# Strassen FFN weights: sums W11+W12 and W11+W12+W22 built by loads and accumulating transfers, W11 loaded by itself

## The chip, the cores and the metric

One core of a Trainium2 chip runs the whole program. The metric is the device time of one execution in microseconds (us), the median of the runs shown. Beside the plain runs there is one profiled execution, from which all rows come. Engines are named as in the profile: PE (TensorE, matmuls), DVE (VectorE), ACT (ScalarE), POOL (GpSimd), SP (SyncE). SP issues plain loads, POOL issues transfers that add to their destination while they write it (accumulating transfers).

## What is computed

A two-layer encoder trunk over two groups of 256 tokens with 1024 channels. Each layer is a half-step SwiGLU FFN, a mixer (gated DeltaNet and differential attention) and a second half-step FFN, so the program has four FFNs. All are in float32. The change touches the FFN alone, in its two products with the gate weights wg and the up weights wu (each 1024 x 2816):

```python
def swiglu(x, wg, wu, wd):
    return (jax.nn.silu(x @ wg) * (x @ wu)) @ wd

x = x + 0.5 * swiglu(rmsnorm(x, ffn1_norm[l]), ffn1_wg[l], ffn1_wu[l], ffn1_wd[l])
```

## The kernel before

Each float32 matmul is three matmuls of a high and a low part: high weights with high and low activations, low weights with high activations. `split` (L218) makes the two parts of a weight tile: ACT casts it to the high part `wh` (L226), DVE subtracts that from the tile for the low part `wl` (L228). The parts live in a pool `pw` of four buffer pairs.

**The FFN.** The 22 column blocks (of 128) are worked through in three groups, (0, 8), (8, 16) and (16, 22). Two blocks at a time make 256 gate and 256 up columns for 512 tokens. The first pair of an FFN uses plain products; each later pair is one call of `seven` (L393), which takes gate and up columns together as a 2 x 2 block matrix and needs seven products instead of eight, by Strassen's scheme: rows 0 to 511 of wg are W11, of wu W12; rows 512 to 1023 of wg are W21, of wu W22. There are ten calls in an FFN (three, four and three in the groups), 40 in the program. After a group comes its part of the down projection with wd (`rowproj`, L298 to L304), some 44 us for eight blocks.

**One call of `seven`** (L393 to L443). A product is 24 matmuls of 256 columns (L389 to L391). In the order of the code the products use W11 (with X11, activations), W11+W12+W22 (called t2), W11+W12, W12+W22 (t3, in the tiles P and M), W21 (in R and S), W22, and W11+W12+W22+W21 (t2 again, after W21 was added). C holds combinations of the activations, made once for each FFN by `combos` (L355 to L374): four tiles of tag u are filled by an SP load of the high parts (L361) and a POOL accumulation of the low parts (L362), then combined by DVE (L363) and split by ACT and DVE (L370, L371).

**How the weights come in before the change.** SP loads W11 into one half of a `raw` tile and W22 into the other (L399, L400), W22 once more in halves into P and M (L403), and W21 in halves into R and S (L407). POOL adds W12 to P and M (L404). W11 is split for the first product; then POOL adds W12 to it in place (L412), which therefore has to wait for that split. DVE adds W22 to the result for t2 (L414).

**What sets the order.** The program is scheduled at build time by a planner that orders every engine's instructions by their priority and by when they can run in its own model; on the chip each engine and each issuing queue then keeps that order. `high_priority(offset=AHEAD)` with AHEAD = 1500 moves loads, splits and the two sums far ahead of their place in the code. How far they really go ahead is set by buffers: two for `raw` (which the loads of wd use too), two each for the tags P, M, R and S, 14 for the tag u. Of these 14, four hold the tokens x, two a call's results hh and hl (until the down projection has read them), one a t2, and for a while four the combinations.

Of the kernel before, what the change touches and what calls it, by code (L numbers as in the profile page):

```python
# [17 lines left out]
ALU = mybir.AluOpType  # L18
# [3 lines left out]
P = 128  # L22
# [12 lines left out]
AHEAD = 1500  # L35
# [25 lines left out]
def trunk_kernel(tc, I, O, dbg=None, depth=DEPTH, stop=None):  # L61
    nc = tc.nc
    with ExitStack() as st:
# [15 lines left out]
        def nm(s):  # L79
            cnt[0] += 1  # L80
            return f"{s}{cnt[0]}"

        def u(shape=(P, 2, TOK), dt=F32):
            return pu.tile(list(shape), dt, tag="u", name=nm("u"))
# [4 lines left out]
        def tmp(shape=(P, TOK)):  # L89
            return pt.tile(list(shape), F32, tag="t", name=nm("t"))  # L90

        def dtmp(tag, shape=(P, H, P)):
            return pd.tile(list(shape), F32, tag=tag, name=nm(tag))
# [4 lines left out]
        def bank(k, shape=(P, TOK)):  # L98
            return {"f": psf, "a": psx, "d": psd}[k].tile(list(shape), F32, tag="b", name=nm("ps"))
# [7 lines left out]
        V, A, G_, T = nc.vector, nc.scalar, nc.gpsimd, nc.tensor  # L107
# [110 lines left out]
        def split(rv, dst=None, share=False, off=AHEAD):  # L218
            shp = list(rv.shape)
            if dst is None:  # L220
                hi = pw.tile(shp, F32R, tag="whi", name=nm("wh"))
                lo = pw.tile(shp, F32R, tag="wlo", name=nm("wl"))
            else:
                hi, lo = dst
            with tc.high_priority(offset=off):
                A.copy(hi, rv)  # L226
                turn[0] += 1
                (G_ if share and turn[0] % 2 else V).tensor_tensor(lo, rv, hi.bitcast(F32), op=ALU.subtract)  # L228
            return hi, lo
# [109 lines left out]
        def ffn(wg, wu, wd, xT, after, extra=None, norm=None):  # L339
# [12 lines left out]
            X11, X12 = [[t[:, k, g0] for t in xT] for k in (low, high)]  # L352
            C = {}
# [22 lines left out]
            def parts_of(pieces):  # L376
                hi = pw.tile([P, 4, 256], F32R, tag="whi", name=nm("wh"))
                lo = pw.tile([P, 4, 256], F32R, tag="wlo", name=nm("wl"))
                n = 4 // len(pieces)
                for i, r in enumerate(pieces):  # L380
                    split(r, (hi[:, n * i:n * i + n, :], lo[:, n * i:n * i + n, :]))
                return hi, lo

            def product(ps, w, act, start=True):
                (wh, wl), (ch, cl) = w, act
                for j in range(2):
                    m, o = slice(j * P, (j + 1) * P), ps[:, j, :]
                    for k in range(4):
                        T.matmul(o, wh[:, k, m], ch[:, k, :], start=start and j + k == 0, stop=False, skip_group_check=True)  # L389
                        T.matmul(o, wh[:, k, m], cl[:, k, :], start=False, stop=False, skip_group_check=True)  # L390
                        T.matmul(o, wl[:, k, m], ch[:, k, :], start=False, stop=k == 3, skip_group_check=True)  # L391

            def seven(f, hh, hl):  # L393
                c = slice(f * P, f * P + 256)
                rows = lambda w, k0, n: w[k0 * P:(k0 + n) * P, c].rearrange("(k p) n -> p k n", p=P)
                with tc.high_priority(offset=AHEAD):
                    r = pr.tile([P, 2048], F32, tag="raw", name=nm("raw")).rearrange("p (q k n) -> p q k n", q=2, k=4)
                    w11, w22 = r[:, 0], r[:, 1]
                    nc.sync.dma_start(w11, rows(wg, 0, 4))  # L399
                    nc.sync.dma_start(w22, rows(wu, 4, 4))  # L400
                    t3 = [dtmp(n, (P, 2, 256)) for n in "PM"]
                    for i, t in enumerate(t3):
                        nc.sync.dma_start(t, rows(wu, 4 + 2 * i, 2))  # L403
                        G_.dma_start(t, rows(wu, 2 * i, 2), accum_op=ALU.add)  # L404
                    w21 = [dtmp(n, (P, 2, 256)) for n in "RS"]
                    for i, t in enumerate(w21):
                        nc.sync.dma_start(t, rows(wg, 4 + 2 * i, 2))  # L407
                sq_ = (P, 2, 256)
                X, E, Z = bank("f", sq_), bank("d", sq_), bank("a", sq_)
                product(X, parts_of([w11]), X11)  # L410
                with tc.high_priority(offset=AHEAD):
                    G_.dma_start(w11, rows(wu, 0, 4), accum_op=ALU.add)  # L412
                    t2 = u((P, 4, 256))
                    V.tensor_tensor(t2, w11, w22, op=ALU.add)  # L414
                p1s, G = dtmp("C", sq_), dtmp("E", sq_)
                A.copy(p1s, X)
                product(E, parts_of([t2]), C[6])
                V.tensor_tensor(G, E, p1s, op=ALU.subtract)
                product(Z, parts_of([w11]), C[5])
                product(E, parts_of(t3), C[7], False)  # L420
                H, y22 = dtmp("B", sq_), tmp(sq_)
                V.tensor_tensor(H, E, p1s, op=ALU.subtract)
                V.tensor_tensor(y22, Z, H, op=ALU.add)
                product(X, parts_of(w21), X12, False)
                s0 = tmp(sq_)
                A.activation(s0, X, AF.Silu)
                with tc.high_priority(offset=AHEAD):
                    for i, t in enumerate(w21):
                        V.tensor_tensor(t2[:, 2 * i:2 * i + 2, :], t2[:, 2 * i:2 * i + 2, :], t, op=ALU.add)
                product(Z, parts_of([w22]), C[3], False)  # L430
                V.tensor_tensor(G, Z, G, op=ALU.add)
                V.tensor_tensor(s0, s0, G, op=ALU.mult)
                product(E, parts_of([t2]), C[4], False)
                y21 = dtmp("B", sq_)
                V.tensor_tensor(y21, p1s, E, op=ALU.subtract)
                A.activation(y21, y21, AF.Silu)
                V.tensor_tensor(y22, y21, y22, op=ALU.mult)
                for v, g in ((s0, g0), (y22, g1)):
                    hi, lo = hh[-1][:, :, g], hl[-1][:, :, g]
                    A.copy(hi, v)  # L440
                    V.tensor_tensor(lo, v, hi.bitcast(F32), op=ALU.subtract)

            for f0, f1 in ((0, 8), (8, 16), (16, 22)):  # L443
                hh, hl = [], []
                for f in range(0, f1 - f0, 2):
                    hh.append(u(dt=F32R))
                    hl.append(u(dt=F32R))
                    if f0 + f:
                        seven(f0 + f, hh, hl)
                        continue  # L450
                    bs = [bank_alt() for _ in range(4)]
                    if norm is not None:
                        ws = []
                        norm(0)
                        for i, (b, rv) in enumerate(zip(bs, raw0)):
                            hi = pw.tile([P, 8, P], F32R, tag="whi", name=nm("wh"))
                            lo = pw.tile([P, 8, P], F32R, tag="wlo", name=nm("wl"))
                            if i:
                                k = (3, 7, 7)[i - 1]
                                A.copy(hi[:, 0, :1], xT[0][:, k, :1])  # L460
                                V.tensor_copy(lo[:, 0, :1], xT[1][:, k, :1])
                            ws.append(split(rv, (hi, lo), off=0 if i else AHEAD))
                            proj(b, ws[-1], xT, 0, 256)
                        norm(1, [w[0][:, 0, :1].bitcast(F32) for w in ws])
                        for b, w in zip(bs, ws):
                            proj(b, w, xT, 256, 512)
                    else:
                        gs, us = wcols(wg, 0), wcols(wu, 0)
                        for g in range(2):
                            for b, w in zip(bs, (gs[0], us[0], gs[1], us[1])):  # L470
                                proj(b, w, xT, g * 256, g * 256 + 256)
                    combos()
                    for j in range(2):
                        gate(bs[2 * j], bs[2 * j + 1], f + j, hh, hl)
# [733 lines left out]
```

## Time and profile before

| | us |
|---|---|
| median of 3 runs | 2539.91 |
| lowest and highest run | 2536.48 and 2541.99 |
| the profiled execution | 2534.26 |
| its span, first to last instruction | 2532.1 |

| engine | busy us | share of the span |
|---|---|---|
| PE | 2357.6 | 93% |
| DVE | 1498.2 | 59% |
| ACT | 1000.4 | 40% |
| POOL | 415.7 | 16% |

The mean granted clock of TensorE is 0.96 of full speed. Transfers move 301.59 MB, 119 GB/s over the span. Matmuls are pipelined and overlap in the records (a matmul of 256 columns stands with 0.28 us while the next one starts 0.12 us later), so the busy time of PE tells little; the distance of the starts does. DMA-issuing instructions are not counted as busy time of an engine.

### The profile page before, as it was taken

Reading aid. Unit: us, or ns where it says so; the run is one execution under the profiler, and the core shown is the slowest. Engines: PE = TensorE matmul, PEld = TensorE weight load, DVE = VectorE, ACT = ScalarE, POOL = GpSimd, SP = SyncE. Lnnn points to the kernel's source line nnn. Section 1 sums busy time; section 2 is a strip of 40 time slices with the busy share of each in tenths; the row PEclk is TensorE's granted clock in tenths of the full one; section 3 lists DMA queues with packets and bytes.
Section 4 is the critical chain, followed back from the end, with each engine's and each line's share of the span. In section 5 each row is a group of like instructions: output and inputs, shape, how many; then the busy total and the mean of one; then the engine's idle time right before and its main releaser. Section 6 shows DMA issues by size and latency. Waiting matters only on the chain.

```text
span 2532.1 us, 36917 instructions
## 1 busy us (share of the span) xinstructions
PE 2357.6 (93%) x14923; PEld 2133.0 (84%) x14923; DVE 1498.2 (59%) x2304; ACT 1000.4 (40%) x1864; POOL 415.7 (16%) x371
## 2 busy tenths in 40 slices
PE   6899999999999979999978989999999999799998
PEld 5888888877799878888878888988878988788897
DVE  4646565577665456564646474655776553656555
ACT  4423344643433334342433242447344333333333
POOL 2101010023351010110011010001333401101000
PEclk8899999999999989999989999999999999899999
DMA  9446435641124375453466454357221245544542
GB/s 228 116 119 132 117 93 183 154 119 57 59 67 142 110 149 142 107 138 98 125 134 139 117 115 124 83 178 182 89 80 46 80 151 136 121 119 111 132 99 76
DMA packets 274842, 301.59 MB, mean 119 GB/s; under 512 B 20589, under 2 KB 240001, under 8 KB 274672
## 3 DMA queue, kind: packets, MB, share of 16 engines
q1 hardware_dynamic: 217888, 230.36, 29.4%
q0 software_dynamic: 56608, 68.68, 16.2%
q8 instruction: 117, 1.92, 0.3%
q14 instruction: 53, 0.43, 0.1%
q10 hardware_dynamic: 176, 0.20, 0.0%
HBM read 271.11 MB, written 11.30 MB: 112 GB/s over the span
## 4 chain that ended last, share of the span: by engine, by line
PE 75%; DVE 11%; DMA 6%; ACT 4%; issue 3%; POOL 1%; SPq 1%; POOLq 0%; DVEq 0%; ACTq 0%
PE ps L389 10%; PE ps L391 10%; PE ps L390 10%; PE ps L298 7%; PE ps L299 7%; PE ps L300 7%; PE ps L241 4%; PE ps L240 4%; PE ps L242 4%; DVE wl L228 2%; DMA u<-xth 2%; ACT wh L226 2%; PE ps L859 1%; DMA v<-gcd 1%; PE ps L956 1%
## 5 line engine op out<-in xcount | busy, mean ns | idle before, releaser
L226 ACT CAST wh<-raw 128x1024 fp32r<-128x1024 f32 x326 | 340.6, 1049 | 584.3 <-PE ps L390 213.2
L228 DVE TENSOR_TENSOR wl<-raw,wh 128x1024 fp32r<-128x1024 f32 x314 | 388.3, 1239 | 285.2 <-ACT wh L226 278.0
L389 PE MATMUL ps<-xth,wh 128*128 128x256 f32 x1280 | 373.2, 292 | 60.7 <-ACT wh L226 58.9
L391 PE MATMUL ps<-xth,wl 128*128 128x256 f32 x1280 | 366.2, 286 | 9.6 <-DVE wl L228 9.6
L390 PE MATMUL ps<-xtl,wh 128*128 128x256 f32 x1280 | 367.8, 287 | 0.0
L389 PE MATMUL ps<-v,wh 128*128 128x256 f32 x960 | 292.7, 305 | 72.5 <-ACT wh L226 70.1
L240 PE MATMUL ps<-xth,wh 128*128 128x512 f32 (+1 forms) x928 | 326.8, 361 | 6.0 <-ACT t L499 2.0
L241 PE MATMUL ps<-xtl,wh 128*128 128x512 f32 (+1 forms) x928 | 329.9, 361 | 1.0 <-DVE xtl L287 1.0
L242 PE MATMUL ps<-xth,wl 128*128 128x512 f32 (+1 forms) x928 | 327.4, 358 | 0.0
L389 PEld LDWEIGHTS ps<-xth,wh 128*128 128x128 f32 x1280 | 251.2, 196 | 68.7 <-ACT wh L226 67.2
L391 PE MATMUL ps<-v,wl 128*128 128x256 f32 x960 | 289.0, 301 | 0.0
L390 PE MATMUL ps<-v,wh 128*128 128x256 f32 x960 | 288.3, 300 | 0.0
L389 PEld LDWEIGHTS ps<-v,wh 128*128 128x128 f32 x960 | 202.1, 210 | 79.1 <-ACT wh L226 75.8
L298 PE MATMUL ps<-wh,u 128*128 128x512 f32 x672 | 261.8, 390 | 0.0
L299 PE MATMUL ps<-wl,u 128*128 128x512 f32 x672 | 261.6, 389 | 0.0
L300 PE MATMUL ps<-wh,u 128*128 128x512 f32 x672 | 259.8, 389 | 0.0
L391 PEld LDWEIGHTS ps<-xth,wl 128*128 128x128 f32 x1280 | 249.1, 195 | 11.0 <-DVE wl L228 11.0
L390 PEld LDWEIGHTS ps<-xtl,wh 128*128 128x128 f32 x1280 | 251.9, 197 | 0.0
L390 PEld LDWEIGHTS ps<-v,wh 128*128 128x128 f32 x960 | 202.2, 211 | 0.4
L391 PEld LDWEIGHTS ps<-v,wl 128*128 128x128 f32 x960 | 202.3, 211 | 0.2
L240 PEld LDWEIGHTS ps<-xth,wh 128*128 128x128 f32 x928 | 174.9, 191 | 32.3 <-ACT xth L286 2.6
L241 PEld LDWEIGHTS ps<-xtl,wh 128*128 128x128 f32 x928 | 177.2, 191 | 24.2 <-DVE xtl L287 1.4
(350 smaller groups left out, 4292.9 us busy)
## 6 DMA issues: line engine op xcount, KB each, us to landing
raw<-in_w_in_dram SPq DMA_DIRECT2D x44, 1024.0 KB, 5.3
raw<-in_ffn_wd_dram SPq DMA_DIRECT2D x40, 1024.0 KB, 6.6
raw<-in_ffn_wg_dram SPq DMA_DIRECT2D x40, 512.0 KB, 4.6
raw<-in_ffn_wu_dram SPq DMA_DIRECT2D x40, 512.0 KB, 5.5
raw<-in_ffn_wu_dram POOLq DMA_DIRECT2D x40, 512.0 KB, 6.0
M<-in_ffn_wu_dram SPq DMA_DIRECT2D x40, 256.0 KB, 2.9
P<-in_ffn_wu_dram SPq DMA_DIRECT2D x40, 256.0 KB, 2.8
M<-in_ffn_wu_dram POOLq DMA_DIRECT2D x40, 256.0 KB, 7.8
```

The source lines that it names most:

```text
L226: A.copy(hi, rv)
L228: (G_ if share and turn[0] % 2 else V).tensor_tensor(lo, rv, hi.bitcast(F32), op=ALU.subtract)
L240: T.matmul(o, wh[:, k, m], xh[:, k, c0:c1], start=k == 0, stop=False)
L241: T.matmul(o, wh[:, k, m], xl[:, k, c0:c1], start=False, stop=False)
L242: T.matmul(o, wl[:, k, m], xh[:, k, c0:c1], start=False, stop=k == n - 1)
L298: T.matmul(ps, sh[:, a], wh, start=k == 0, stop=False)
L299: T.matmul(ps, sh[:, a], wl, start=False, stop=False)
L300: T.matmul(ps, sl[:, a], wh, start=False, stop=k == nk - 1)
L389: T.matmul(o, wh[:, k, m], ch[:, k, :], start=start and j + k == 0, stop=False, skip_group_check=True)
L390: T.matmul(o, wh[:, k, m], cl[:, k, :], start=False, stop=False, skip_group_check=True)
L391: T.matmul(o, wl[:, k, m], ch[:, k, :], start=False, stop=k == 3, skip_group_check=True)
L859: T.matmul(pp[:, h, :], lhs[:, h, :], rhs[:, h, :], start=True, stop=True)
```

## The change

W11 no longer shares a buffer with W11+W12. The half of the `raw` tile where W11 stood (now `t1_`) receives a load of W11 and, as soon as that has landed, POOL's accumulation of W12. W11 by itself is loaded again, in halves, into two tiles of the tag S, and split half by half. The sum t2 is no longer made by DVE: a tile of tag u receives a load of W22 and then two accumulations by POOL, of W12 and of W11. W21 moves from the tags R and S into two tiles of the tag R. For each call this makes nine loads on SP (of 0.26 or 0.52 MB) where there were six, with 3.1 MB instead of 2.1, and five accumulations on POOL where there were three, with 2.1 MB instead of 1.05; one DVE instruction of 128 x 1024 elements (L414) goes.

```diff
                 with tc.high_priority(offset=AHEAD):
                     r = pr.tile([P, 2048], F32, tag="raw", name=nm("raw")).rearrange("p (q k n) -> p q k n", q=2, k=4)
-                    w11, w22 = r[:, 0], r[:, 1]
-                    nc.sync.dma_start(w11, rows(wg, 0, 4))
+                    w11, w22, t1_ = [dtmp("S", (P, 2, 256)) for _ in range(2)], r[:, 1], r[:, 0]
+                    nc.sync.dma_start(t1_, rows(wg, 0, 4))
                     nc.sync.dma_start(w22, rows(wu, 4, 4))
+                    G_.dma_start(t1_, rows(wu, 0, 4), accum_op=ALU.add)
+                    for i, t in enumerate(w11):
+                        nc.sync.dma_start(t, rows(wg, 2 * i, 2))
+                    t2 = u((P, 4, 256))
+                    nc.sync.dma_start(t2, rows(wu, 4, 4))
+                    G_.dma_start(t2, rows(wu, 0, 4), accum_op=ALU.add)
+                    G_.dma_start(t2, rows(wg, 0, 4), accum_op=ALU.add)
                     t3 = [dtmp(n, (P, 2, 256)) for n in "PM"]
                     for i, t in enumerate(t3):
                         nc.sync.dma_start(t, rows(wu, 4 + 2 * i, 2))
                         G_.dma_start(t, rows(wu, 2 * i, 2), accum_op=ALU.add)
-                    w21 = [dtmp(n, (P, 2, 256)) for n in "RS"]
+                    w21 = [dtmp("R", (P, 2, 256)) for _ in range(2)]
                     for i, t in enumerate(w21):
                         nc.sync.dma_start(t, rows(wg, 4 + 2 * i, 2))
                 sq_ = (P, 2, 256)
                 X, E, Z = bank("f", sq_), bank("d", sq_), bank("a", sq_)
-                product(X, parts_of([w11]), X11)
-                with tc.high_priority(offset=AHEAD):
-                    G_.dma_start(w11, rows(wu, 0, 4), accum_op=ALU.add)
-                    t2 = u((P, 4, 256))
-                    V.tensor_tensor(t2, w11, w22, op=ALU.add)
+                product(X, parts_of(w11), X11)
                 p1s, G = dtmp("C", sq_), dtmp("E", sq_)
                 A.copy(p1s, X)
                 product(E, parts_of([t2]), C[6])
                 V.tensor_tensor(G, E, p1s, op=ALU.subtract)
-                product(Z, parts_of([w11]), C[5])
+                product(Z, parts_of([t1_]), C[5])
```

## Rows read from the trace of the kernel before

**Rows 1.** The page, part 4: shares of the chain that ended last, by engine.
```profile
PE 75%; DVE 11%; DMA 6%; ACT 4%; issue 3%; POOL 1%; SPq 1%; POOLq 0%; DVEq 0%; ACTq 0%
```

**Rows 2.** Waits of PE: who waited for whom, us in total, times, longest us.
```profile
PE ps L389 <- ACT wh L226: 129.0, 55, 17.0
```

**Rows 3.** Timeline of PE at a hand-over: start us, us, instruction, count [idle before, releaser].
```profile
1060.16 0.28 PE L390 MATMUL ps<-xtl,wh 128*128 128x256 f32 x1
1060.28 0.28 PE L391 MATMUL ps<-xth,wl 128*128 128x256 f32 x1
1062.18 0.38 PE L389 MATMUL ps<-v,wh 128*128 128x256 f32 x1 [1.62 <-ACT wh L226]
...
1063.92 0.41 PE L390 MATMUL ps<-v,wh 128*128 128x256 f32 x1
1064.13 0.41 PE L391 MATMUL ps<-v,wl 128*128 128x256 f32 x1
```

**Rows 4.** Windows of sevens: bounds, us, engines' busy us, PEclk, DMA share, GB/s; three sums.
```profile
906.20:993.80 87.60, 66.78 (x506) 65.06 (x505) 58.21 (x70) 35.92 (x48) 11.64 (x10) 0.88 0.59 124
...
sum 358.60, PE 268.26 PEld 261.24 DVE 233.42 ACT 146.88 POOL 48.29; mean PE 67.06 PEld 65.31 DVE 58.36 ACT 36.72 POOL 12.07
...
sum 380.30, PE 347.91 PEld 342.51 DVE 242.70 ACT 153.53 POOL 54.29; mean PE 86.98 PEld 85.63 DVE 60.68 ACT 38.38 POOL 13.57
...
sum 279.20, PE 259.10 PEld 255.54 DVE 178.93 ACT 119.03 POOL 27.89; mean PE 64.77 PEld 63.88 DVE 44.73 ACT 29.76 POOL 6.97
```

**Rows 5.** Windows of shorter stretches, columns as in rows 4.
```profile
1030.00:1040.00 10.00, 10.00 (x56) 8.71 (x55) 8.33 (x11) 3.19 (x4) 0.00 (x0) 1.00 0.00 0
...
1062.20:1087.10 24.90, 22.21 (x168) 21.79 (x168) 17.20 (x22) 10.73 (x16) 3.69 (x3) 0.93 0.57 127
...
1070.00:1080.00 10.00, 10.00 (x85) 10.00 (x85) 4.89 (x6) 2.83 (x4) 3.43 (x3) 1.00 0.85 202
```

**Rows 6.** Timelines of DVE and POOL ahead of the same hand-over.
```profile
1050.90 1.21 DVE L228 TENSOR_TENSOR wl<-raw,wh 128x1024 fp32r<-128x1024 f32 x1
...
1059.30 1.22 DVE L414 TENSOR_TENSOR u<-raw 128x1024 f32<-128x1024 f32 x1
...
1052.41 1.30 POOL L412 DMA_DIRECT2D raw<-in_ffn_wu_dram  x1 [7.66 <-DVE wl L228]
```

**Rows 7.** DMA issues: transfer, queue, count, KB each, median us from issue to landing.
```profile
raw<-in_ffn_wg_dram SPq DMA_DIRECT2D x40, 512.0 KB, 4.6
...
raw<-in_ffn_wu_dram POOLq DMA_DIRECT2D x40, 512.0 KB, 6.0
```

**Rows 8.** Timelines of POOL and DVE ahead of a second stretch's first seven.
```profile
1023.86 1.30 POOL L412 DMA_DIRECT2D raw<-in_ffn_wu_dram  x1 [37.85 <-DVE wl L228]
...
1029.84 1.22 DVE L414 TENSOR_TENSOR u<-raw 128x1024 f32<-128x1024 f32 x1 [6.28 <-DMA raw<-in_ffn_wu_dram]
```

**Rows 9.** The page, part 3: queue of SP, queue of POOL: packets, MB, share of 16 engines.
```profile
q1 hardware_dynamic: 217888, 230.36, 29.4%
q0 software_dynamic: 56608, 68.68, 16.2%
```

**Rows 10.** Timelines of DVE (split of combinations) and PE in a first stretch.
```profile
929.67 2.35 DVE L371 TENSOR_TENSOR v<-u,v 128x1024 fp32r<-128x1024 f32 x2
...
946.86 0.28 PE L391 MATMUL ps<-xth,wl 128*128 128x256 f32 x1
```

**Rows 11.** DMA queues from 880 to 915 us, columns as in rows 9.
```profile
q0 software_dynamic: 3027, 3.00, 57.9%
q1 hardware_dynamic: 4622, 4.54, 45.3%
```

**Rows 12.** Timelines of DVE and PE at the start of that first stretch.
```profile
914.03 1.23 DVE L363 TENSOR_TENSOR u<-u,u 128x1024 f32<-128x1024 f32 x1 [12.14 <-DMA u<-xtl]
...
920.30 0.58 PE L389 MATMUL ps<-xth,wh 128*128 128x256 f32 x1 [11.05 <-ACT wh L226]
...
924.45 0.58 PE L391 MATMUL ps<-xth,wl 128*128 128x256 f32 x1 [1.58 <-DVE wl L228]
```

## The prediction

> **What bounds the kernel now.** The page first: three quarters of the chain that ended last are TensorE's own matmuls [rows 1]; a gain must come out of the rest. Next, what TensorE waits for: one entry stands far above all others, 129.0 us in 55 waits of the first matmul of a product for a high part that ScalarE makes at L226 [rows 2]. Third, where these waits lie: the windows of the twelve stretches of sevens (three in each FFN, one for each group of columns before its down projection). Full speed is a matmul every 0.12 us, as at the end of a seven [rows 3], so a seven of 168 matmuls takes 20.16 us. The first stretches of the four FFNs (three sevens each, 60.5 us at full speed) take 358.6 us instead of 241.9, 116.7 too much; the second (four sevens each) 380.3 instead of 322.6, 57.7 too much; the third (three each) 279.2 instead of 241.9, 37.3 too much [rows 4].
>
> In the second and third stretches that loss of 95.0 us lies at the 20 places where one seven hands over to the next, 4.75 us each. Fourth, the timeline at one of them. TensorE has its last matmul at 1060.28, its next at 1062.18, and then another short wait [rows 3]; after the gap matmuls start 0.21 us apart instead of 0.12 [rows 3]. The granted clock is 0.93 over a seven with such a gap and 1.00 from 1070 to 1080, where there is none [rows 5]: behind the idle time TensorE runs for a while at the lower of its two levels (1.2 instead of 2.4 GHz), and this adds about as much as the gap.
>
> The gap is the end of one chain. VectorE finishes the split of W11 at 1052.11; only then may POOL add W12 to the same buffer (issued 1052.41) [rows 6], which lands 6.0 us later at the median [rows 7], at 1058.4. VectorE, meanwhile at the tail of the seven before, starts the sum W11+W12+W22 (L414) at 1059.30 and takes 1.22 us [rows 6]; ScalarE's cast of it (1.05 us) then releases TensorE at 1062.18 [rows 3]. From the split's end to the restart that is 10.1 us.
>
> The counter-example is the first seven of a second stretch. There the transfer went out at 1023.86 and the sum stood at 1031.06, long before its use [rows 8], and TensorE was busy for the whole 10 us from 1030 to 1040, the entry into the stretch among them [rows 5]. **An early sum means no gap.**
>
> **The change, part by part.** *The chain.* After the change the two sums are made from loads and accumulating transfers that wait for no split and no VectorE instruction, only for a buffer. L414 goes (40 times 1.22 us of VectorE, on the path at the hand-overs); the two halves of W11 cost two short casts and two short subtractions where one long one stood, a few tenths of a us, beside products of 2.9 us and four buffer pairs of split weights, so I count that at nothing; without this cover it would be 40 times 0.3, 12 us. What is late next is the split itself, about 2.3 us (1.05 on ScalarE, 1.2 on VectorE); its buffer pair comes free three products, 8.6 us, before it is needed.
>
> *The transfers.* Each seven gains a 0.52 MB load of W22 for the sum, another load of W11, and two accumulations of 0.52 MB more; W11's old place now receives W11+W12. The SP queue's 230.36 MB cost 29.4% of the span, 3.23 us of the sixteen engines for each MB; POOL's 68.68 MB cost 16.2%, 5.97 us for each MB [rows 9]. So a seven gains 1.05 times 3.23 plus 1.05 times 5.97: 3.4 + 6.3 = 9.7 us. It has 0.57 of 24.9, 14.2 us, today [rows 5]. The sum is 23.9 us of transfer for 20.16 us of matmuls.
>
> That gives both ends for the 20 hand-overs. If transfers stay hidden, all 95.0 us come back. If they set the pace, a seven takes 23.9 instead of 24.9, and 20 us come back. In favour of hiding: between stretches lies a down projection of some 44 us in which the engines rest for long (share 0.00 from 1030 to 1040 [rows 5]), and raw weights and the M, P sums of two sevens fit into their buffers ahead. Against: W11 and W21 now have buffers for one seven only (S and R), so their loads start one seven ahead, not two; with 4.6 us for a load [rows 7] they still have some 18 us. The rows are nearer to hiding; I take three quarters of the way, **76 us**.
>
> A rule speaks to this. The Trainium skill, page "DMA: Bandwidth & Descriptors", section "Anatomy of one DMA — SWDGE (gpsimd) path", puts such a transfer at 2.0 us plus its bytes at 436 GB/s, an estimate of 3.2 us for 512 KB. The trace does not agree: 6.0 us at the median [rows 7]. By the page's rate the four added half megabytes would take 4.8 us and not 9.7, a seven 19.0, transfers could set no pace, and rival C would gain weight.
>
> *First stretches, hand-overs.* Their 116.7 us are mostly the wait at the start (next); from 906.2 to 993.8 the start costs about 15 of 27.1 us, the two hand-overs 12, so some 48 in four FFNs. Ends: 0 and 48. The sum's buffer comes from the 14 of tag u: 4 hold x, 4 the combinations of the activations, two a seven its results. If they are handed out in the order in which the code asks, the second seven's sum gets one that the combinations leave, at 932.0 at the latest [rows 10]. One load (4.6) and two accumulations (6.0 each [rows 7]) make 16.6, so 948.6, while TensorE runs dry at 947.0 [rows 10]: little gain there, a good one at the hand-over after it. I take **20 us**.
>
> *First stretches, starts.* After a norm the combinations go through transfers too: they land at 914.0, and TensorE, idle for 11.05 us before 920.30, goes on steadily at 924.45 [rows 12]. From 880 to 915 the two queues already take 57.9% and 45.3% of the engines [rows 11]. Into that time falls the first sum: 0.52 MB of load and 1.05 MB of accumulation, 1.7 + 6.3 = 8.0 us. W11+W12 no longer waits for the split and can go out ahead of that time, and the next seven's takes its place. If all of it goes ahead of the combinations, each of four starts loses 8 us, 32 in all. Behind the landing, L414 and a split that waited for it go, up to 5 us each, 20 in all. Between −20 and +32 I take the middle, **+8 us**; POOL's queue, which now holds a second accumulation that waits for the first, speaks for the loss, and the moved W11+W12 for the gain.
>
> Everything else (down projections, the mixers) keeps its instructions.
>
> **Sum.** −76 − 20 + 8 = −88 us. The profiled execution took 2534.26 us (span 2532.1 and 2.2 around it), 5.7 below the median of the runs, 2539.91; taken off the median, 2452.
>
> **Rivals.** (A) *Transfers set the pace.* 20 us at the hand-overs, 10 in the first stretches, 16 lost at the starts: −14, 2526. For it: 23.9 against 20.16, and 103% of the engines in use from 880 to 915 [rows 11]. Against it: the long rests above. The Trainium skill, same page, section "Issuing engines are not separate DMA queues", lets transfers from all issuing engines share the same sixteen DMA engines: by it the work taken from VectorE comes back as transfer time, and the 103% agree.
>
> (B) *Slower: chained transfers that cannot be packed.* Load, accumulation, accumulation is a row of three landings, with POOL's and SP's queues in order behind each wait. Where transfers crowd, the engines still reach only about 0.85 (1070 to 1080 [rows 5]), so a seven would take 23.9/0.85 = 28.1 us, 3.2 more than now: 20 times 3.2, plus 32 at the starts, +96, 2636. It decides from the point where a seven takes over 24.9, that is below 96% of packing while the stretch's lead is used up. Against it: a stretch has three or four sevens, and enters with a good part of two loaded.
>
> (C) *Everything vanishes*: −95 − 48 − 20 = −163, 2377.
>
> (D) *The sums come no earlier*, because their buffers of tag u come free as late as VectorE's add ran: every hand-over keeps its gap, 2540. Against it: from the second stretch on the buffers of the products before come free during the down projection.
>
> **How the numbers follow.** Forecast 0.62, C 0.12, A 0.11, B 0.10, D 0.05. The range leaves out B, D and most of C: 2400 to 2530. A measurement of this kernel tells 0.2% (5 us) from no change: faster 0.84 (forecast, C, nearly all of A), same 0.05, slower 0.11.
>
> **What would show it.** Right: the wait of L389's successor for L226 falls from 129.0 to under 70 us, second stretches from 95 to some 85 us; POOL's queue carries about 111 MB, SP's 272, with shares near 26% and 35%; TensorE's granted clock rises above 0.96. Wrong: sevens of 24 us or more with ScalarE waiting for a transfer of u or raw (A, B), or starts that grow by over 8 us. If the sums still land behind the tail of the seven before, D holds.

## The result, and the profile after

| | before | after |
|---|---|---|
| median of 3 runs, us | 2539.91 | 2823.17 |
| lowest and highest run, us | 2536.48, 2541.99 | 2820.98, 2826.73 |
| ratio of the times, 95% interval | | 1.113 (1.111 to 1.115) |
| span of the profiled execution, us | 2532.1 | 2818.9 |
| mean granted clock of TensorE | 0.96 | 0.91 |

The changed kernel is 11% slower, where 3.5% faster was forecast. The lines that answer to the rows of before come from five views. First the page: part 3 (queues of SP and POOL: packets, MB, share of 16 engines) and part 4 (shares of the chain that ended last; compare [rows 1, 9]).

```profile
q1 hardware_dynamic: 260768, 272.31, 30.9%
q0 software_dynamic: 98848, 110.62, 24.2%
...
PE 60%; DMA 21%; DVE 8%; issue 5%; ACT 3%; SPq 1%; POOL 1%; POOLq 0%; DVEq 0%; ACTq 0%
```

The bytes are those of the prediction (272 and 111 MB). But transfers, 6% of the chain before, are 21% now. Next the waits (who for whom: us, times, longest us; compare [rows 2]):

```profile
PE ps L389 <- ACT wh L226: 409.3, 46, 17.6
...
ACT wh L226 <- DMA u<-in_ffn_wg_dram: 274.7, 32, 14.7
```

TensorE's wait for ScalarE's cast has grown from 129.0 to 409.3 us, and the cast itself waits 274.7 us for a transfer from wg into a tile of u: that is t2's last accumulation (L407 now). The windows of the twelve stretches, second FFN's second stretch and the three sums (columns as in [rows 4]):

```profile
1134.80:1260.00 125.20, 88.22 (x674) 86.73 (x673) 57.19 (x76) 38.76 (x56) 20.03 (x16) 0.84 0.65 148
...
sum 443.70, PE 276.23 PEld 269.46 DVE 222.09 ACT 151.50 POOL 74.00; mean PE 69.06 PEld 67.36 DVE 55.52 ACT 37.88 POOL 18.50
...
sum 495.40, PE 354.86 PEld 348.86 DVE 229.25 ACT 156.07 POOL 79.88; mean PE 88.72 PEld 87.21 DVE 57.31 ACT 39.02 POOL 19.97
...
sum 351.40, PE 260.02 PEld 255.96 DVE 167.70 ACT 119.51 POOL 43.25; mean PE 65.01 PEld 63.99 DVE 41.92 ACT 29.88 POOL 10.81
```

First, second and third stretches took 358.6, 380.3 and 279.2 us before; they now take 85.1, 115.1 and 72.2 us more, 272.4 of the 286.8 us by which the span has grown. (Another 13.3 us lie ahead of the first FFN's first seven, below.) The transfers are not what is full: their share in the window is 0.65. At 26 of the 28 hand-overs TensorE now stands still for 9 to 14 us (at the other two for 5.4 and 16.9), and the granted clock in this window is 0.84.

Where a stretch loses it shows in the timelines of one hand-over (start us, us, instruction [idle before, releaser]); DVE, SP, POOL, ACT, PE one after the other:

```profile
1147.57 0.68 DVE L228 TENSOR_TENSOR wl<-S,wh 128x512 fp32r<-128x512 f32 x1
...
1148.77 0.68 DVE L228 TENSOR_TENSOR wl<-S,wh 128x512 fp32r<-128x512 f32 x1
...
1148.28 1.57 SPq L403 DMA_DIRECT2D S<-in_ffn_wg_dram  x2
1149.94 0.43 SPq L405 DMA_DIRECT2D u<-in_ffn_wu_dram  x1
...
1158.28 1.28 POOL L406 DMA_DIRECT2D u<-in_ffn_wu_dram  x1 [8.12 <-PE ps L391]
1164.22 1.28 POOL L407 DMA_DIRECT2D u<-in_ffn_wg_dram  x1 [4.67 <-DMA u<-in_ffn_wu_dram]
...
1170.05 1.04 ACT L226 CAST wh<-u 128x1024 fp32r<-128x1024 f32 x1 [10.95 <-DMA u<-in_ffn_wg_dram]
...
1171.15 0.58 PE L389 MATMUL ps<-v,wh 128*128 128x256 f32 x1 [13.19 <-ACT wh L226]
```

Read from the bottom: TensorE restarts 1.1 us after the cast starts, the cast at once when the last accumulation has landed, this starts when the one before has landed, and that when t2's load (L405) has landed. (The bracket at L406 names a product, L391. But L405 took 7.8 us to land, until 1157.7, and in the list of waits L406 stands mostly with this load:)

```profile
POOL u L406 <- DMA u<-in_ffn_wu_dram: 313.1, 32, 32.4
```

The load leaves SP at 1149.94. On SP it stands right behind the two halves of W11 for the **next** seven (L403), and these wait for the split of this seven's W11: its subtractions end at 1148.25 and 1149.45, and the two halves leave at 1148.28 and just behind the second. So the three landings hang on the split again. From its end to the restart it is now 21.7 us, where it was 10.1 us in the kernel before.

No buffer holds that load at this place. In the built program its tile of u was the low part of a result of the first group before; the last to read such a part is the down projection, which is over when this stretch starts at 1134.80. And in the list of SP's waits L403 stands with 162.9 us for the split, L405 not at all:

```profile
SPq L403 <- DVE wl L228: 162.9, 71, 5.5
```

### The profile page after: what moved, and what is told of

Its sections match the earlier page's. It is cut to its first block, busy times and chain, and to the rows that moved or that the text cites. A ratio compares the mean times of both kernels' runs of the same rounds, so it can differ in the third digit from the quotient of the medians.

```text
span 2818.9 us, 37399 instructions
## 1 busy us (share of the span) xinstructions
PE 2376.6 (84%) x14923; PEld 2149.7 (76%) x14923; DVE 1460.1 (52%) x2304; ACT 1007.1 (36%) x1904; POOL 518.1 (18%) x451
## 3 DMA queue, kind: packets, MB, share of 16 engines
q1 hardware_dynamic: 260768, 272.31, 30.9%
q0 software_dynamic: 98848, 110.62, 24.2%
## 4 chain that ended last, share of the span: by engine, by line
PE 60%; DMA 21%; DVE 8%; issue 5%; ACT 3%; SPq 1%; POOL 1%; POOLq 0%; DVEq 0%; ACTq 0%
DMA u<-in_ffn_wu_dram 11%; PE ps L389 7%; PE ps L298 7%; PE ps L299 7%; PE ps L300 7%; PE ps L391 6%; PE ps L390 6%; DMA u<-in_ffn_wg_dram 6%; PE ps L241 3%; PE ps L240 3%; PE ps L242 3%; DVE wl L228 2%; ACT wh L226 2%; DMA u<-xth 1%; PE ps L862 1%
## 5 line engine op out<-in xcount | busy, mean ns | idle before, releaser
L389 PE MATMUL ps<-v,wh 128*128 128x256 f32 x960 | 303.1, 316 | 394.4 <-ACT wh L226 394.4
L389 PEld LDWEIGHTS ps<-v,wh 128*128 128x128 f32 x960 | 211.0, 220 | 401.2 <-ACT wh L226 400.9
L226 ACT CAST wh<-raw 128x1024 fp32r<-128x1024 f32 x286 | 299.1, 1048 | 503.2 <-PE ps L390 171.7
L228 DVE TENSOR_TENSOR wl<-raw,wh 128x1024 fp32r<-128x1024 f32 x274 | 340.1, 1244 | 245.1 <-ACT wh L226 239.5
L391 PE MATMUL ps<-xth,wl 128*128 128x256 f32 x1280 | 359.4, 284 | 0.0
L390 PE MATMUL ps<-v,wh 128*128 128x256 f32 x960 | 296.5, 309 | 0.0
L228 DVE TENSOR_TENSOR wl<-u,wh 128x1024 fp32r<-128x1024 f32 x80 | 98.0, 1225 | 382.1 <-ACT wh L226 382.0
L391 PE MATMUL ps<-v,wl 128*128 128x256 f32 x960 | 295.7, 308 | 0.1
L389 PEld LDWEIGHTS ps<-xth,wh 128*128 128x128 f32 x1280 | 249.9, 195 | 27.4 <-ACT wh L226 27.4
L300 PE MATMUL ps<-wh,u 128*128 128x512 f32 x672 | 260.9, 389 | 0.0
L390 PEld LDWEIGHTS ps<-xtl,wh 128*128 128x128 f32 x1280 | 251.0, 196 | 0.0
L391 PEld LDWEIGHTS ps<-xth,wl 128*128 128x128 f32 x1280 | 245.1, 193 | 0.2 <-DVE wl L228 0.2
L226 ACT CAST wh<-u 128x1024 fp32r<-128x1024 f32 x80 | 83.8, 1047 | 377.2 <-DMA u<-in_ffn_wg_dram 274.7
L390 PEld LDWEIGHTS ps<-v,wh 128*128 128x128 f32 x960 | 211.4, 220 | 0.3
L391 PEld LDWEIGHTS ps<-v,wl 128*128 128x128 f32 x960 | 209.8, 219 | 0.7 <-DVE wl L228 0.7
```

The costliest lines, as they stand in the source:

```text
L300: T.matmul(ps, sl[:, a], wh, start=False, stop=k == nk - 1)
```

## The experiments

Three theories, named as in the expectations, which were written before each run. **Q**, the order of the queues: t2's load stands in SP's queue behind something that waits for the split; its own inputs and buffer are ready. **U**: on the chip t2 gets its buffer of tag u no earlier. **T**: the transfers themselves, or their sum, set the pace. The stretches of all kernels that ran (us, sums of four windows each, as in [rows 4]). Each experiment ran beside the kernel before, whose median was then 2535 to 2537 us; the ratios below go by these.

| kernel | median | first | second | third |
|---|---|---|---|---|
| before | 2539.91 | 358.6 | 380.3 | 279.2 |
| after | 2823.17 | 443.7 | 495.4 | 351.4 |
| e1_touch | 2421.61 | 328.9 | 322.7 | 243.9 |
| e2_w11act | 2792.60 | 440.8 | 486.1 | 341.5 |
| e3_t2dve | 2544.19 | 353.4 | 380.9 | 284.3 |
| e4_dve_touch | 2450.02 | 318.4 | 349.1 | 255.4 |
| e5_bef_touch | 2468.07 | 358.2 | 378.8 | 276.3 |
| e6_first_early | 2394.14 | 301.2 | 322.6 | 244.0 |
| e7_two_early | 2408.03 | 297.9 | 322.7 | 243.9 |
| e8_one_acc | 2655.18 | 381.0 | 431.9 | 299.5 |
| e9_load_only | 2540.40 | 358.4 | 374.3 | 285.5 |

At full speed the three sums would be 241.9, 322.6 and 241.9.

**e1_touch: the same transfers in another order.**

```diff
+                    for t in (hh[-1], hl[-1]):
+                        V.memset(t[:, 0, :1].bitcast(F32), 0.0)
                     t3 = [dtmp(n, (P, 2, 256)) for n in "PM"]
```

Why two memsets move a load: in the built programs t2's load stands right where the planner has placed the first write of the seven before into its hl, also a tile of u. It looks as if the planner hands out the buffers of a tag in the order of the first writes in the code, so that t2's has to wait (in the plan) for a result of the seven before. A first write far ahead frees the order. The planner's rule is inferred from this effect; the orders were read from the built programs.

> The changed kernel, with two one-column memsets on VectorE for each call of seven (first columns of hh and hl, written over later). They are there only to let the build-time planner hand out the buffers of tag u in another order: in the program that it now builds, SP's load for t2 stands ahead of the next seven's halves of W11 instead of behind them. Transfers and arithmetic are otherwise the same. Theory Q (the queue's order: t2's three landings start only behind the split of the same seven's W11): the waits of about 11 us before the second product of a seven go at nearly all 28 hand-overs, 2450 to 2550 us. Theory U (on the chip t2 has no free buffer of tag u any earlier): as the changed kernel, 2790 to 2830 us. Theory T (the transfers themselves set the pace): a seven takes 23.9 to 28.1 us instead of some 29, 2500 to 2680 us, and ScalarE then waits for raw and S as well as for u.

It took 2421.61 us, ratio to before 0.954 (0.952 to 0.956): Q, and a little better. Of its views, the waits of PE, SP's load of t2 for the hand-over shown above, then a window and the sums of the second and third stretches:

```profile
PE ps L389 <- ACT wh L226: 84.3, 7, 19.6
```

```profile
990.30 0.37 SPq L405 DMA_DIRECT2D u<-in_ffn_wu_dram  x1
```

```profile
1006.40:1087.10 80.70, 80.70 (x674) 80.67 (x673) 56.55 (x80) 38.41 (x56) 19.95 (x16) 1.00 1.01 231
...
sum 322.70, PE 322.70 PEld 322.62 DVE 226.12 ACT 153.58 POOL 77.21; mean PE 80.67 PEld 80.65 DVE 56.53 ACT 38.40 POOL 19.30
...
sum 243.90, PE 243.84 PEld 243.16 DVE 173.92 ACT 122.35 POOL 29.27; mean PE 60.96 PEld 60.79 DVE 43.48 ACT 30.59 POOL 7.32
```

This load leaves 16.1 us ahead of its stretch (which starts at 1006.40); in the changed kernel it left 15.1 us behind the start (1149.94, start at 1134.80). The second and third stretches run at full speed, 322.7 for 322.6 and 243.9 for 241.9. U and T, for this place, fall: with the same bytes in the same pools the sevens take 20.2 us. A buffer does hold SP's loads of t2 at times here (the list of SP's waits names the readers in the down projection, L300), and no stretch loses by it:

```profile
SPq L405 <- PE ps L300: 105.3, 20, 8.5
```

**e2_w11act: W11 off SP's queue.**

```diff
-                        nc.sync.dma_start(t, rows(wg, 2 * i, 2))
+                        A.dma_start(t, rows(wg, 2 * i, 2))
```

> The changed kernel, with the two loads of W11 (tag S) issued from ScalarE's queue instead of SP's. SP's load for t2 then no longer stands behind a load that waits for the split of W11, but still behind the next seven's two raw loads, which wait for the split of W22 of the seven before, some 14 us ahead of the hand-over. Theory Q: three landings of about 20 us against some 17 us of lead instead of 11.5: the wait falls from about 11 to 3 us a hand-over, 2480 to 2620 us. Theory U: no change, 2790 to 2830 us. Theory T: 2500 to 2680 us with ScalarE waiting for several kinds of transfers.

A miss: 2792.60 us, what U expected. The timelines of DVE, SP and PE at a hand-over:

```profile
1163.52 1.23 DVE L228 TENSOR_TENSOR wl<-raw,wh 128x1024 fp32r<-128x1024 f32 x1 [0.26 <-ACT wh L226]
...
1164.77 0.37 SPq L399 DMA_DIRECT2D raw<-in_ffn_wg_dram  x1
1165.19 0.52 SPq L400 DMA_DIRECT2D raw<-in_ffn_wu_dram  x1
1165.79 0.60 SPq L405 DMA_DIRECT2D u<-in_ffn_wu_dram  x1
...
1190.35 0.58 PE L389 MATMUL ps<-v,wh 128*128 128x256 f32 x1 [10.80 <-ACT wh L226]
```

The place is as Q had it: L405 follows the raw loads, which start 0.02 us after the split of W22 (ending 1164.75). The sizes were not. The loads now leave all together, and this one takes 10.6 us to land, so from the split's end to the restart it is 25.6 us; and the split of W22 ends 14.8 us before TensorE runs dry (at 1179.55), where 17 were expected. The gap of 10.8 us is the difference. To move one of two waiting loads off the queue is worth little, 31 us. By itself this run can't tell Q from U.

**e3_t2dve and e4_dve_touch: half of the change, in either order.** In e3 VectorE makes t2 again; e4 adds the memsets of e1.

```diff
-                    nc.sync.dma_start(t2, rows(wu, 4, 4))
-                    G_.dma_start(t2, rows(wu, 0, 4), accum_op=ALU.add)
-                    G_.dma_start(t2, rows(wg, 0, 4), accum_op=ALU.add)
+                    V.tensor_tensor(t2, t1_, w22, op=ALU.add)
```

> Half of the change: W11+W12 by a load and an accumulating transfer into raw, W11 by itself in halves, W21 in tag R; but t2 is again made by VectorE from W11+W12 and W22, with no load and no accumulation of its own. The prediction's step (the hand-over's gap of the kernel before ends with the accumulation that had to wait for the split of W11): the 20 gaps go, 2440 to 2470 us. Theory Q (VectorE's order: the planner puts this sum behind the last instructions of the seven before, whatever its inputs do): the gaps stay, 2520 to 2560 us, as the kernel before.

> As e3_t2dve, with the two one-column memsets of e1_touch, so that VectorE's sum for t2 stands earlier in VectorE's order, ahead of the end of the seven before. Theory Q: the gaps of the kernel before at the 20 hand-overs of second and third stretches go, and part of those in first stretches, 2400 to 2470 us. Theory U: no buffer any earlier, so the sum still starts behind the tail of the seven before, 2520 to 2560 us. Theory T: one load more than the kernel before for a seven, so at most 1 to 2 us a seven, below 2540 us in any case.

e3 took 2544.19 us, 1.003 of before (1.002 to 1.005), stretches included: the gaps stay. The accumulation of W12 for this seven left at 1024.06 and landed 5.9 us later, at 1030 (POOL's timeline, and the landing in the list for L401 in that window):

```profile
1024.06 1.28 POOL L401 DMA_DIRECT2D raw<-in_ffn_wu_dram  x1 [12.47 <-issue]
```

```profile
DMA to landing us min/median/max: 5.9/5.9/5.9
```

The sum started 26 us after that, without idle time before it, behind a low part of the seven before (L442), as L414 in [rows 6]; DVE's timeline:

```profile
1055.46 0.69 DVE L442 TENSOR_TENSOR u<-t,u 128x512 fp32r<-128x512 f32 x1
1056.07 1.22 DVE L405 TENSOR_TENSOR u<-raw 128x1024 f32<-128x1024 f32 x1
```

So it was VectorE's order, and not the accumulation, that ended the gap of the kernel before. e4 gives the sum an early place and takes 2450.02 us, 0.965 (0.962 to 0.968); the second and third stretches are 55 us shorter than before.

**e5_bef_touch: the kernel before, with the memsets alone** (the two lines of e1, ahead of `p1s`).

> The kernel before, with nothing of the change, but with the two one-column memsets of e1_touch, so that VectorE's sum W11+W12+W22 (L414) stands ahead of the end of the seven before in VectorE's order. The accumulation of W12 still waits for the split of W11. Theory Q: the split comes some 8.6 us and three products ahead of the hand-over, 11.5 us ahead of the use; accumulation 6.0, sum 1.2 and cast 1.05 make 8.3 us, so the gaps go without the change, 2430 to 2470 us, about as e4_dve_touch. The prediction's step (the chain of 10.1 us behind the split sets the gap, and only transfers free of the split remove it): the gaps stay, 2515 to 2545 us.

2468.07 us, 0.972 (0.971 to 0.974): Q's upper end. 69 us of e1's gain need nothing of the change. (Its stretches look long because most hold 21 matmuls of the down projection now, 694 in a second stretch where there were 673; at a distance of 0.23 us these are 4.8 us a stretch. So the memsets moved other work too, and 69 us is what they give in all.) Now the sum does wait for the accumulation that waits for the split, 6.40 us, and TensorE 0.37 us for the cast (DVE's and PE's timelines):

```profile
1033.32 1.23 DVE L414 TENSOR_TENSOR u<-raw 128x1024 f32<-128x1024 f32 x1 [6.40 <-DMA raw<-in_ffn_wu_dram]
...
1035.73 0.39 PE L389 MATMUL ps<-v,wh 128*128 128x256 f32 x1 [0.37 <-ACT wh L226]
```

That is the chain that the prediction saw, at its own price: 0.4 us at this hand-over, 2.8 at the last of the same stretch.

**e8_one_acc and e9_load_only: the chain made shorter, the order left alone.** From the changed kernel e8 takes the accumulation of W11 (L407), e9 that of W12 (L406) too.

```diff
                     nc.sync.dma_start(t2, rows(wu, 4, 4))
-                    G_.dma_start(t2, rows(wu, 0, 4), accum_op=ALU.add)
-                    G_.dma_start(t2, rows(wg, 0, 4), accum_op=ALU.add)
```

> The changed kernel with the order of its queues as it is, but t2's last accumulation (of W11) left out, so the kernel computes with W12+W22 in place of W11+W12+W22: one landing of three is taken off the chain. Theory Q (three landings of some 20 us in a row behind the split of W11, which gives 11.5 us of lead): each of 28 hand-overs and 4 starts loses a landing of 5.8 us less and some of the lower clock behind it, so 190 to 260 us come back: 2565 to 2635 us. Theory T (the transfers' sum sets the pace): half a megabyte of accumulation a seven, 3.1 us, 125 us in all: 2700 us.

> As e8_one_acc, with both accumulations of t2 left out, so the kernel computes with W22 in place of W11+W12+W22: one landing is left of three. Theory Q: a load of 6 to 8 us and a cast of 1.0 fit into the 11.5 us behind the split, the gaps go: 2420 to 2480 us, though the load still stands behind the halves of W11. Theory T: 6.3 us a seven, 250 us: 2570 us.

2655.18 us (1.046 of before, 1.043 to 1.049) and 2540.40 us (1.002, 1.001 to 1.004). One landing less is worth 168 us, a second 115. The first lies between the two expectations (Q 190 to 260, T 125); the second ended 60 us above Q's range and 30 below T's time. The two together, 283 us, lie nearer to T's 250 than to Q's range, so by themselves they don't tell Q from T; e1, with all the transfers at full speed, does. What is left in e9 is again an order, ScalarE's. At one hand-over the load left at 1045.13 and took 6.3 us, so it was there at 1051.4; its cast stands behind two instructions that wait for the seven before and for this seven's first product (L417). ACT's and PE's timelines:

```profile
1053.19 0.59 ACT L417 COPY C<-ps 128x512 f32<-128x512 f32 x1 [0.84 <-PE ps L391]
1053.67 0.62 ACT L441 CAST u<-t 128x512 fp32r<-128x512 f32 x1
1054.19 1.05 ACT L226 CAST wh<-u 128x1024 fp32r<-128x1024 f32 x1
...
1055.29 0.39 PE L389 MATMUL ps<-v,wh 128*128 128x256 f32 x1 [2.14 <-ACT wh L226]
```

Before, e3 and e9 make t2 in three ways and take 2540, 2544 and 2540 us: as long as it has that late place, what it is made of counts only when its chain is longer than the place allows.

**e6_first_early and e7_two_early: the starts.** What e1 still loses lies in the first stretches. In the second FFN's start TensorE stands for 18.4 us for t2 (PE's timeline of e1, then that of e6 below):

```profile
902.24 0.58 PE L389 MATMUL ps<-v,wh 128*128 128x256 f32 x1 [18.41 <-ACT wh L226]
```

The loads are split off `seven` as `load(f)`; e7 has the last line too.

```diff
+                    first[2] = load(2)
+                    touch(hh, hl)
+                    first[4] = load(4)
                     combos()
```

> e1_touch, with the loads and accumulations of an FFN's first seven written in the code ahead of the combinations of the activations, and with hh and hl of the first pair touched there too. In e1_touch TensorE stands still for some 18 us in each of the four starts, for this t2, whose load stands behind the combinations' and behind the halves of W11 of the next seven. Theory Q: t2 is there before the combinations are; what then ends the wait is the combinations, some 3 to 5 us after the first product. That gives back 10 to 15 us a start: 2360 to 2390 us. Theory T (so close to the start the sixteen engines are full, and what goes ahead of the combinations delays them by as much): 2405 to 2435 us, as e1_touch.

> e6_first_early, with the loads and accumulations of the second seven written ahead of the combinations as well. Theory Q: any wait left at the first hand-over of a first stretch goes, up to 5 us a start, 2345 to 2390 us. Theory T: two sevens' transfers ahead of the combinations delay these by some 8 us a start more, 2390 to 2440 us.

e6: 2394.14 us, 0.944 (0.942 to 0.945), 27.5 less than e1, 27.7 of it in the first stretches; 4 us above Q's range. The wait in that start is 9.26 us now, and ends with a combination:

```profile
882.96 0.58 PE L389 MATMUL ps<-xth,wh 128*128 128x256 f32 x1 [9.26 <-ACT xth L370]
```

e7: 2408.03 us, 0.949 (0.948 to 0.951), slower than e6 by 14 although its first stretches are 3 us shorter: the first matmul of the second FFN's stretch comes at 886.5 instead of 870.7. That looks like T, transfers put ahead of the combinations that delay them. But half of the 15.8 us stands already at a step of the norm ahead of it (L247 at 847.36, in e6 at 839.50), and most of the rest goes with an order again, POOL's (its timeline in e7):

```profile
862.58 1.27 POOL L407 DMA_DIRECT2D u<-in_ffn_wg_dram  x1 [6.84 <-DMA u<-in_ffn_wu_dram]
863.36 1.08 POOL L247 TENSOR_TENSOR nr<-nst,mhalf 128x1 f32<-128x1 f32 x1
863.88 1.95 POOL L362 DMA_DIRECT2D u<-xtl  x1
```

t2's second accumulation waits 6.84 us for the landing of the first, and behind it stand the next step of the norm, which moves no data by DMA, and the next accumulation of the combinations. Whether T adds to this is not shown. e6 is the fastest of all these kernels.

## Why the prediction was wrong

- **What bounds the kernel.** TensorE's wait for the cast of t2 and the gaps at the hand-overs: right, and e1 gave back 92.9 of the 95.0 us that the second and third stretches lost. Who ended the gap: wrong. L414 in [rows 6] has no bracket, so VectorE was not idle before it; a late landing would have left one, as [rows 8] shows (6.28 <-DMA). In the whole trace of before L414 waits for this transfer nine times (VectorE's waits), at the first start and at the eight entries into a second or third stretch; at the hand-overs VectorE's idle time before it is 0.11 us at most:

```profile
DVE u L414 <- DMA raw<-in_ffn_wu_dram: 62.8, 9, 11.6
```

  The accumulation did land just ahead of it, at 1058.4, and what came after it was taken for its effect.
- **The step that failed: the sums "wait for no split and no VectorE instruction, only for a buffer".** True of the data; false of the queue. SP's load for t2 came to stand behind a load that waits for the split (162.9 us of waits at L403), and t2's cast and load took the late place that L414 had, now with three landings behind it, 21.7 us, instead of one sum. The prediction named queues in order behind each wait, in rival B, but looked up no place in them. Rival D had the mechanism nearest to it, a sum that comes no earlier because of tag u, and its price wrong: not the same gap, 2540, but one of mostly 9 to 14 us at the hand-overs, where the order in the plan and not a free buffer on the chip decides. Rival B had the direction and the row of three landings, and took its price, +96, from crowding, which is not what costs here. The prediction's own rows would have given the price (an estimate): load and two accumulations, 16.6 us, and the cast, 1.05, are 17.7 us behind the same split where 10.1 stood, 7.6 us more at each of 28 hand-overs, some 210 us. It made 21.7 us, and 272.4 in the stretches.
- **Transfers.** The price was right: in e1 35.8% of 2422.6 us for 272.31 MB is 3.19 us for each MB on SP's queue, 27.8% for 110.62 MB 6.09 on POOL's (taken: 3.23 and 5.97). The 23.9 us of a seven set no pace: of the 95.6 us of four, e1 moves 81.5 in its stretch (80.7 at a share of 1.01) and so the rest ahead of it, and TensorE waits for none. The three quarters taken for the hand-overs (76 us) could have been all. Rival A is excluded there; rival B's chained landings do take longer in a crowd, and cost e1 nothing at the hand-overs. The sign set for A and B (sevens of 24 us or more, ScalarE waiting for a transfer of u) did come out, 31 us a seven in the second stretches and 274.7 us of waits, and still neither is the cause: the sign doesn't tell a late start from a slow transfer.
- **First stretches.** Predicted −20 at the hand-overs and +8 at the starts, −12; e1, with the sums early, has −29.7, the changed kernel +85.1.
- **Left out: W11's new tag.** W11 now goes into tag S, which the norm uses for its own tiles, and its load stands on SP behind combinations. In the first FFN it leaves at 33.59 us instead of 12.55 (when it went to raw) and takes 18.7 us to land, and the first matmul of the stretch comes at 52.94 instead of 39.6, 13.3 us later (e1: 12.2); e5, with W11 in raw, has it at 39.6. SP's and PE's timelines of the changed kernel:

```profile
31.40 2.10 SPq L361 DMA_DIRECT2D u<-xth  x1
33.59 6.21 SPq L403 DMA_DIRECT2D S<-in_ffn_wg_dram  x2
...
52.94 0.58 PE L389 MATMUL ps<-xth,wh 128*128 128x256 f32 x1 [12.95 <-ACT wh L226]
```

  The splitting into halves, counted at nothing, is not seen to cost anything.
- **The sum.** e1's stretches give −29.7 − 57.6 − 35.3, and +12.2 at the first start, −110.4; its span is 109.5 us shorter. The forecast's −88 was a fair estimate of a kernel in which these sums are early. The changed kernel isn't that one; and of such a gain 69 us come without the change (e5). With the order mended in both, the change is worth another 46 us (2421.61 against 2468.07).

## What to carry to other kernels

A step that loses its data dependences is not yet early: look up where it stands in the order of each engine and queue that it goes through, and what the instruction ahead of it waits for. A row without idle time before it says that the order was the limit; before a chain is rebuilt, give its step an earlier place as a trial (here two memsets of one column for each call of seven, 69 us). And a chain of transfers in place of one sum is cheap while it is early, and costs each of its landings in full when it is late.

## What the runs showed of the hardware

The share of DMA can be over 1, at full speed of TensorE; e1, one seven in the middle of a stretch:

```profile
1023.80:1044.00 20.20, 20.20 (x171) 20.20 (x170) 15.40 (x23) 10.19 (x15) 5.06 (x4) 1.00 1.10 214
```

So the times of the packets overlap in the records, and a share of 1 isn't the end of what fits into a stretch. What a crowd does to one transfer is seen in the landings. The accumulation of W12 into t2 takes 5.9 us at the median in the changed kernel and 8.1 in e1 (DMA issues of each kernel: transfer, queue, count, KB, median us):

```profile
u<-in_ffn_wu_dram POOLq DMA_DIRECT2D x40, 512.0 KB, 5.9
```

```profile
u<-in_ffn_wu_dram POOLq DMA_DIRECT2D x40, 512.0 KB, 8.1
```

The Trainium skill, page "DMA: Bandwidth & Descriptors", section "Issuing engines are not separate DMA queues", has all issuing engines share the sixteen DMA engines; the longer landings agree with it.
